# Two transformer blocks on one core: shorter norm chains, row sums on their own timer and queue, earlier weight splits, and the second mixer's norm chain issued inside its output projection

## The chip, the core and the metric

One core of a Trainium2 chip runs the whole program. Its engines each have a queue of their own and meet by semaphores: TensorE (PE) for matrix products and transposes, VectorE (DVE), ScalarE (ACT), GpSimd (POOL) and SyncE (SP, which issues DMAs). The metric is the device time of one execution in microseconds (us), the median of several runs. A trace of one execution, the profile, is at hand.

## What is computed

Two blocks, one after the other, over 256 positions of width 1024, all in float32. The first: a gated feed-forward (inner width 2816), a mixer with two attention branches, a second feed-forward. The second: a mixer with three branches (an mLSTM scan, a differential attention, a state space scan) that also looks at a 256-long context, and a feed-forward with a three-tap convolution over positions. Between them stands the residual with its norms:

```python
def rms_norm(x, g):
    xf = x.astype(jnp.float32)
    y = xf * lax.rsqrt(jnp.mean(xf * xf, axis=-1, keepdims=True) + EPS)
    return (y * g.astype(jnp.float32)).astype(x.dtype)

h = h + 0.5 * rms_norm(swiglu(rms_norm(h, ffn1_pre_g), ...), ffn1_post_g)
h = h + rms_norm(hybrid_mixer(rms_norm(h, mix_pre_g), ...), mix_post_g)
h = h + 0.5 * rms_norm(swiglu(rms_norm(h, ffn2_pre_g), ...), ffn2_post_g)
```

The second block is modulated: from the vector c six rows of 1024 are made, `silu(c) @ w_mod + b_mod` ("rows" below), which scale, shift and gate the normed input. `modulate(h, shift, scale)` is `h * (1 + scale) + shift`.

## The kernel before, in words

**Products.** Each float32 operand is split into a high and a low part in the fast format float32r; a product is three matmuls, hi x hi, hi x lo and lo x hi (lines 355 to 357 of `mm3`). Activations are kept transposed, `xT`, 128 features by 256 positions. A projection tile of 256 columns is 2 x 24 matmuls of about 0.12 us each. Expansions (`ffn_up`, `proj_fm`) write to PSUM from `psB`, `down` sums the result over all tiles for both blocks of 128 positions (`acc[tb]`, tb 0 and 1).

**Weights.** Class `Weights` loads pieces of 512 KB (`raw`, 5 buffers, SP's queue, L111) and splits each: `wh` on ACT (L126), `wl` on DVE (L127), into a ring of 4. `ahead` fills the ring as far as it may; `presplit` splits further pieces into general buffers (`u`).

**Order.** The order of all instructions is written out by hand: a clock counts the products that were issued (`tick`), and generators ("sides") are stepped when their time has come. In each tick the sides that were just made go first, then `ahead`, then the others. So an engine's queue holds weight splits, norm steps and row steps in the order of these ticks, and each waits in line. `heads` steps the attention heads of a mixer, in the first mixer every 2.6 us of this clock.

**The norm chains.** `residual_norm` makes the new residual and the next block's input: for each tb a generator `chain`, and a list `order` of what to step in each tick (0 and 1: the chains; 2 and 3: `to_T` of tb 0 and 1, eight transposes at L511, then hi on ACT at L346 and lo on DVE at L347). A chain squares on ACT with a running sum (L435), adds the two halves on DVE (L437), makes mean + eps (L421), takes the power -1/2 on POOL (L427), and scales on DVE (L459, L477, L479; L473 is the premultiplication by the gain where there is a shift; L456 and L464 multiply by the gain behind the down projection). While it runs, projections of the context (`ctx_attn`, `ctx_mlstm`, `ctx_ssd`) give TensorE work, one tick for each 24 products.

**The rows.** `mod_rows` is a side that adds up w_mod tiles on DVE (L981, L983), a step every `pace` us of the clock; after eight of them a generator `reduced` splits the sum (L346, L347), multiplies it by ones on TensorE (L957), adds bias and gain (L959, L961) and writes the row to DRAM. Its small DMAs go by SP; w_mod comes by ACT's queue (L975) into `v`, the pool of 12 buffers of 512 columns that heads and chains use, too.

**The second mixer** runs its heads in three groups, four mLSTM heads, eight attention steps and eight state space heads; `decay` (L1094 to L1107) makes for each scan head two tiles in `v`. Behind it `down("w_out_2", ...)` projects, and its norm chain is issued when that is through.

## Time and profile before

| | |
|---|---|
| median of three runs | 1230.99 us (1229.41 to 1232.49) |
| the profiled execution | 1230.0 us, its span 1228.2 us |
| busy TensorE, VectorE, ScalarE, GpSimd | 96%, 75%, 51%, 6% of the span |
| matmul instructions | 8728 |
| mean granted clock of TensorE | 0.989 of full speed |
| DMA | 251.33 MB, mean 205 GB/s |

The span runs from the first to the last instruction; the 1.8 us beside it lie around it. A row of a timeline gives the start in us, the duration, the engine, the line, the operation, what it writes and reads and how often, and in brackets the engine's idle time before it with what ended it. Starts of TensorE's rows are good, their ends are modelled. The granted clock is the share of full speed that TensorE was given; it has two levels, 1.2 and 2.4 GHz.

### The profile page before, as it was taken

How to read it: one execution, taken by the hardware profiler on the slowest of the kernel's cores; microseconds unless marked ns; L12 is line 12 of the kernel's file. 1: busy time of each engine (PE TensorE's matmuls, PEld its weight loads, DVE VectorE, ACT ScalarE, POOL GpSimd, SP SyncE). 2: the span in 40 equal slices, each digit the busy share in tenths (PEclk: the TensorE clock that was granted, in tenths of full speed). 3: DMA queues.
4: the chain of work that ended last, by engine and by line, in shares of the span. 5: the costliest groups of instructions: out<-in, count | busy, mean ns of one | idle time of the engine just before them, and what ended most of it. 6: DMA issues, size and time to landing. Idle time of an engine off the chain costs nothing. (4 is left out here: it accounts for less than half of the span.)

```text
span 1228.2 us, 22195 instructions
## 1 busy us (share of the span) xinstructions
PE 1184.8 (96%) x8728; PEld 1110.4 (90%) x8728; DVE 925.5 (75%) x1596; ACT 622.7 (51%) x1063; POOL 67.7 (6%) x84
## 2 busy tenths in 40 slices
PE   7999999998999988999999999999999998999998
PEld 7999988898978978999988899999898997999887
DVE  5798856666667869889886976698668777888854
ACT  4454545545556455454454654555566353555542
POOL 0020000100000000000000100055000000000000
PEclk8999999999999999999999999999999999999999
DMA  7888687576334776788888455446423384555572
GB/s 273 273 262 269 199 309 254 157 263 223 127 127 138 235 285 224 248 273 271 267 295 331 133 176 181 137 139 191 136 78 112 113 284 154 179 180 172 172 263 80
DMA packets 80644, 251.33 MB, mean 205 GB/s; under 512 B 9542, under 2 KB 10870, under 8 KB 80540
## 3 DMA queue, kind: packets, MB, share of 16 engines
q1 hardware_dynamic: 61692, 215.85, 52.0%
q10 hardware_dynamic: 18432, 33.56, 8.3%
q8 instruction: 68, 1.11, 0.4%
q0 software_dynamic: 416, 0.50, 0.3%
q14 instruction: 36, 0.29, 0.1%
HBM read 241.46 MB, written 8.42 MB: 203 GB/s over the span
## 5 line engine op out<-in xcount | busy, mean ns | idle before, releaser
L127 DVE TENSOR_TENSOR wl<-raw,wh 128x1024 fp32r<-128x1024 f32 (+3 forms) x358 | 423.6, 1218 | 129.6 <-ACT wh L126 124.9
L355 PE MATMUL pB<-u,wh 128*128 128x256 f32 x1696 | 486.2, 287 | 0.9 <-ACT u L346 0.9
L357 PE MATMUL pB<-u,wl 128*128 128x256 f32 x1696 | 482.0, 284 | 1.0 <-DVE wl L127 1.0
L356 PE MATMUL pB<-u,wh 128*128 128x256 f32 x1696 | 481.5, 284 | 0.8 <-DVE u L347 0.7
L126 ACT ACTIVATE wh<-raw 128x1024 fp32r<-128x1024 f32 (+3 forms) x358 | 358.8, 1046 | 97.5 <-PE pA L357 22.3
L355 PEld LDWEIGHTS pB<-u,wh 128*128 128x128 f32 x1696 | 326.5, 192 | 9.5 <-issue 7.2
L357 PEld LDWEIGHTS pB<-u,wl 128*128 128x128 f32 x1696 | 326.5, 193 | 2.3 <-DVE wl L127 1.4
L356 PEld LDWEIGHTS pB<-u,wh 128*128 128x128 f32 x1696 | 326.5, 193 | 2.0 <-DVE u L347 1.5
L355 PE MATMUL pB<-wh,u 128*128 128x512 f32 (+3 forms) x614 | 208.2, 339 | 1.6 <-ACT wh L126 1.6
L356 PE MATMUL pB<-wl,u 128*128 128x512 f32 (+3 forms) x614 | 206.9, 337 | 1.0 <-DVE wl L127 0.9
L357 PE MATMUL pB<-wh,u 128*128 128x512 f32 (+3 forms) x614 | 206.3, 336 | 0.0
L355 PEld LDWEIGHTS pB<-wh,u 128*128 128x128 f32 x614 | 117.4, 191 | 13.3 <-ACT wh L126 1.8
L356 PEld LDWEIGHTS pB<-wl,u 128*128 128x128 f32 x614 | 117.3, 191 | 13.3 <-DVE wl L127 2.5
L357 PEld LDWEIGHTS pB<-wh,u 128*128 128x128 f32 x614 | 117.1, 191 | 11.8
L519 ACT ACTIVATE w<-pB 128x256 f32<-128x256 f32 x44 | 16.9, 384 | 114.1 <-PE pB L357 113.7
L427 POOL TENSOR_TENSOR rs<-ms,nhalf 128x1 f32<-128x1 f32 (+2 forms) x30 | 29.2, 975 | 815.3 <-DVE ms L421 812.6
L983 DVE SCALAR_TENSOR_TENSOR v<-v,silu_c,v 128x512 f32<-128x512 f32 x84 | 62.4, 743 | 0.3
L1010 DVE SCALAR_TENSOR_TENSOR w<-pB,cols,w 128x255 f32<-128x255 f32 x120 | 49.6, 476 | 15.9 <-ACT w L1005 10.1
L520 DVE SCALAR_TENSOR_TENSOR w<-w,pB 128x256 f32<-128x256 f32 x44 | 18.5, 419 | 30.2 <-ACT w L519 30.2
L356 PE MATMUL pA<-wl,u 128*128 128x256 f32 x132 | 38.3, 290 | 1.8 <-DVE wl L127 1.8
L355 PE MATMUL pA<-wh,u 128*128 128x256 f32 x132 | 38.6, 292 | 0.9 <-ACT wh L126 0.9
L357 PE MATMUL pA<-wh,u 128*128 128x256 f32 x132 | 37.9, 287 | 0.0
(363 smaller groups left out, 1322.3 us busy)
## 6 DMA issues: line engine op xcount, KB each, us to landing
raw<-f_gu SPq DMA_DIRECT2D x88, 512.0 KB, 5.4
v<-w_mod ACTq DMA_DIRECT2D x128, 256.0 KB, 4.9
raw<-w_lat SPq DMA_DIRECT2D x64, 512.0 KB, 4.1
raw<-f_dn SPq DMA_DIRECT2D x44, 512.0 KB, 5.7
raw<-w_up_t SPq DMA_DIRECT2D x44, 512.0 KB, 5.1
raw<-w_ctx SPq DMA_DIRECT2D x22, 512.0 KB, 5.0
raw<-w_down_t SPq DMA_DIRECT2D x22, 512.0 KB, 5.1
raw<-w_in_g SPq DMA_DIRECT2D x16, 512.0 KB, 4.6
```

What stands on the lines that cost most here:

```text
L126: nc.scalar.activation(hi, r, AF.Copy)
L127: nc.vector.tensor_tensor(out=lo, in0=r, in1=hi.bitcast(F32), op=OP.subtract)
L355: nc.tensor.matmul(out, a[0], b[0], start=first, stop=False)
L356: nc.tensor.matmul(out, a[0], b[1], start=False, stop=False)
L357: nc.tensor.matmul(out, a[1], b[0], start=False, stop=last)
L427: self.nc.gpsimd.tensor_tensor(out=r, in0=ms, in1=self.nhalf[:, :width], op=OP.pow)
L519: nc.scalar.activation(th, p[:, 0], AF.Tanh, scale=0.5)
L520: nc.vector.scalar_tensor_tensor(th, th, 1.0, p[:, 0], op0=OP.add, op1=OP.mult)
L983: nc.vector.scalar_tensor_tensor(acc, ws[n - ahead], sc, acc, op0=OP.mult, op1=OP.add)
L1010: nc.vector.scalar_tensor_tensor(y[j][:, o], p[:, j, x], tap(t, i), y[j][:, o], op0=OP.mult, op1=OP.add)
```

## The change

- **Pools:** `v` has 10 buffers instead of 12; w_mod tiles get a pool of 5.
- **Norm chains:** squares are scaled so that their sums are means (`mean2`), and one DVE step adds both with eps (`rstd2`), where there were two. The chain with a norm has one more yield, and the orders interleave the two blocks otherwise and put the transposes a tick later.
- **Start:** the first gain comes as one row and is spread by TensorE; the second block's squares are taken on DVE; fewer warm-up products.
- **Heads:** the first step comes one pace after `heads` is called.
- **Rows:** each half's reduction is a side of its own, with two pauses of 2 us and then one tick from load and product to the addition; its small DMAs go by POOL's queue. In the second and third norm stage the row side is held off by 14 us. `need_rows` steps these sides too. The pace is 2.5 instead of 2.6 in the second feed-forward.
- **Early splits:** one piece each in two tiles of `w_out_t` and of the second `f2_dn`, two pieces at the last but one tile of the last expansion. The last `down` takes tb 0's sums from `psA` and tb 1's from `psB`.
- **Second mixer:** a hook in `down("w_out_2", ...)` issues tb 0's whole chain ahead of tb 1's last products, the first part of tb 1's chain and tb 0's transposes ahead of tb 1's last 256 columns, and the rest of tb 1's chain behind the products; tb 1's sums are in three parts (512, 256, 256). The end of `down`, `ahead`, comes after that, then tb 1's transposes.

```diff
-NV = 12
+NV = 10
...
-        side = self.side(run())
+        side = self.side(run(), pace)
...
+    def down(self, name, nt, hT, aside=None, late=1, cols=((512, 512), (512, 512)), first=None, hook=None):
+        ps = lambda tb, n: first if first and tb == 0 else self.psB if first or n == 512 else self.psA
+        acc = [[ps(tb, n)([128, n]) for n in cols[tb]] for tb in range(TB)]
...
+            order = [(k, *x) for k in range(2) for x in each] if i or first else [(k, *x) for x in each for k in range(2)]
...
         for tb in range(TB):
             for x in range(len(cols[tb])):
+                if hook:
+                    hook(acc, tb, x)
                 for m in range(late):
                     for k in range(2):
                         mm(w, k, 2 * (nt - late + m) + k, tb, x, m)
+        if hook:
+            hook(acc, TB, 0)
         self.weights.ahead()
...
+    def mean2(self, src):
+        nc, got = self.nc, []
+        for x in src:
+            got.append(self.sb([128, 1], "ssq", 8))
+            nc.scalar.activation(self.v([128, 512])[:, :x.shape[-1]], x, AF.Square, scale=D ** -0.5, accum_out=got[-1])
+        return got
+
+    def rstd2(self, m):
+        nc = self.nc
+        e, r = self.sb([128, 1], "mse", 6), self.sb([128, 1], "rs1", 6)
+        nc.vector.scalar_tensor_tensor(e, m[0], EPS, m[1], op0=OP.add, op1=OP.add)
+        nc.gpsimd.tensor_tensor(out=r, in0=e, in1=self.nhalf[:, :1], op=OP.pow)
+        return r
...
-    def residual_norm(self, acc, h, gpost, norm, gpre, shift, xT, order=((0, 0), (1,), (0, 1), (2,), (1,), (3,))):
+    def residual_norm(self, acc, h, gpost, norm, gpre, shift, xT, order=((0, 0, 1, 0, 1), (1, 0), (1,), (), (2,), (), (3,)), mid=None):
...
             if norm:
-                s = self.sumsq(acc[tb])
+                r = self.rstd2(self.mean2(acc[tb]))
+                yield
                 for hf in range(2):
                     nc.vector.tensor_tensor(out=x[hf], in0=acc[tb][hf], in1=self.halves(gpost)[hf], op=OP.mult)
-                r = self.rstd(s, D, 1)
+                yield
                 for hf in range(2):
                     nc.vector.scalar_tensor_tensor(y[hf], x[hf], r, y[hf], op0=OP.mult, op1=OP.add)
-                yield
-                s = self.sumsq(y)
+                m = self.mean2(y)
+                yield
             elif acc is not None:
+                m, c = [], 0
+                for a in acc[tb]:
+                    cc, c = slice(c, c + a.shape[-1]), c + a.shape[-1]
+                    nc.vector.tensor_tensor(out=t[tb][:, cc], in0=a, in1=gpost[:, cc], op=OP.mult)
+                    nc.vector.tensor_tensor(out=h[tb][:, cc], in0=t[tb][:, cc], in1=h[tb][:, cc], op=OP.add)
+                    m += self.mean2([h[tb][:, cc]])
+                    if len(m) == 3:
+                        s = self.sb([128, 1], "ssq", 8)
+                        nc.vector.tensor_tensor(out=s, in0=m[0], in1=m[1], op=OP.add)
+                        m = [s, m[2]]
+                    yield
+            elif tb:
+                m = []
                 for hf in range(2):
+                    m.append(self.sb([128, 1], "ssq", 8))
+                    nc.vector.scalar_tensor_tensor(x[hf], y[hf], 1.0 / D, y[hf], op0=OP.mult, op1=OP.mult, accum_out=m[-1])
             else:
-                s = self.sumsq(y)
-            r = self.rstd(s, D, 1)
+                m = self.mean2(y)
+            r = self.rstd2(m)
...
-            yield
+            if not norm:
+                yield
...
-    def ffn_up(self, name, xT, act):
+    def ffn_up(self, name, xT, act, early=0):
...
+            if f == NFF - 2:
+                self.weights.presplit(early)
...
         def reduced(acc, c, j, gain, hf):
             hi, lo = self.v([128, 512], F32R), self.v([128, 512], F32R)
             self.split(hi, lo, acc)
+            yield 2
+            yield 2
             x = self.v([1, 512])
-            nc.sync.dma_start(x, I["b_mod_2"][:, j * D + hf * 512:j * D + hf * 512 + 512])
+            nc.gpsimd.dma_start(x, I["b_mod_2"][:, j * D + hf * 512:j * D + hf * 512 + 512])
...
-            yield
             p = self.psA([128, 512])
...
-            nc.sync.dma_start(self.rows[c, j][:, hf * 512:hf * 512 + 512], x)
+            nc.gpsimd.dma_start(self.rows[c, j][:, hf * 512:hf * 512 + 512], x)
...
-                ws.append(self.v([128, 512]))
+                ws.append(self.sb([128, 512], "wm", 5))
...
-                    half.append(reduced(acc, c, j, gain, hf))
+                    half.append(self.side(reduced(acc, c, j, gain, hf)))
+                    self.row_sides = half[-2:]
...
+        gain = self.u([1, D])
+        nc.sync.dma_start(gain, I["ffn1_pre_g"])
...
-        self.warm_up(17)
-        t = self.residual_norm(None, h, None, False, g, None, xT, ((0, 0, 1), (1, 2), (3,)))
+        self.warm_up(4)
+
+        g, gain2 = self.u([128, D]), [self.psA([128, 512]) for _ in range(2)]
+        for hf in range(2):
+            nc.tensor.matmul(gain2[hf], self.ones[:1], self.halves(gain)[hf], start=True, stop=True)
+        self.warm_up(8)
...
+        t = self.residual_norm(None, h, None, False, g, None, xT, ((0, 1, 4, 0, 1, 2), (3,)), gains1)
...
-        acc = self.down("w_out_t", 4, mT)
+        acc = self.down("w_out_t", 4, mT, lambda i: self.weights.presplit(1) if i else None)
...
+        rows.ready += 14
...
-        pace[0] = 2.6
+        pace[0] = 2.5
...
+            if i in (8, 9):
+                self.weights.presplit(1)
...
-        t = self.residual_norm(acc, h, gp["post"], True, gp["pre"], gp["shift"], xT)
+        rows.ready += 14
+        t = self.residual_norm(acc, h, gp["post"], True, gp["pre"], gp["shift"], xT, ((0, 0, 1, 0, 1), (1, 0), (1,), (), (2,), (3,)))
...
-        acc = self.down("w_out_2", 4, mT, lambda i: self.weights.presplit(2 * i), 2)
-        t = self.residual_norm(acc, h, gp["post"], False, gp["pre"], gp["shift"], xT, ((0, 0, 0, 1, 1, 1, 0, 1, 2, 3),))
+        def hook(acc, tb, x):
+            if (tb, x) == (1, 0):
+                side.append(self.residual_norm(acc, h, gp["post"], False, gp["pre"], gp["shift"], xT,
+                                               ((0, 0, 0, 0), (1, 2), (1, 1, 1, 1), (3,))))
+            elif (tb, x) in ((1, 2), (2, 0)):
+                side[0].step()
+
+        self.down("w_out_2", 4, mT, lambda i: self.weights.presplit(2 * i), 2, ((512, 512), (512, 256, 256)), hook=hook)
+        self.join(*side)
...
-        hT = self.ffn_up("w_up_t", xT, self.conv_silu_mul)
+        hT = self.ffn_up("w_up_t", xT, self.conv_silu_mul, 2)
...
-        acc = self.down("w_down_t", NFF // 2, hT, None, 2, cols)
+        acc = self.down("w_down_t", NFF // 2, hT, None, 2, cols, first=self.psA)
```

## Rows read from the trace of the kernel before

**Rows 1.** Page, part 1: busy time, share of the span and instructions of each engine

```profile
PE 1184.8 (96%) x8728; PEld 1110.4 (90%) x8728; DVE 925.5 (75%) x1596; ACT 622.7 (51%) x1063; POOL 67.7 (6%) x84
```

**Rows 2.** Table of stretches: busy us (instructions), granted clock, DMA share, GB/s

```profile
220.00:240.00 20.00, 19.91 (x155) 19.67 (x155) 10.74 (x16) 10.19 (x17) 0.55 (x1) 0.91 0.42 138
...
300.00:320.00 20.00, 16.16 (x112) 15.71 (x111) 13.10 (x25) 6.13 (x13) 0.00 (x0) 0.83 0.40 133
...
480.00:500.00 20.00, 19.90 (x167) 19.48 (x166) 18.93 (x30) 9.94 (x17) 0.00 (x0) 1.00 0.82 281
```

**Rows 3.** Timeline of PE: start, us, form, count [idle before <- who ended it]

```profile
220.09 1.77 PE L511 MATMUL pB<-ident,u 128*128 128x128 f32 x8 [2.80 <-DVE u L477]
...
304.48 1.91 PE L829 MATMUL pA<-ident,u 128*96 128x128 f32 x8 [3.84 <-DVE u L690]
...
450.32 0.39 PE L356 MATMUL pA<-wl,u 128*128 128x256 f32 x1 [0.88 <-DVE wl L127]
...
463.63 1.97 PE L511 MATMUL pB<-ident,u 128*128 128x128 f32 x8 [3.91 <-DVE u L477]
...
687.80 1.32 PE L511 MATMUL pB<-ident,u 128*128 128x128 f32 x8 [1.76 <-DVE u L479]
...
1026.79 3.34 PE L511 MATMUL pB<-ident,u 128*128 128x128 f32 x16 [4.51 <-DVE u L479]
...
1166.95 0.50 PE L355 MATMUL pB<-wh,u 128*128 128x512 f32 x1 [1.57 <-ACT wh L126]
...
1168.21 0.50 PE L356 MATMUL pB<-wl,u 128*128 128x512 f32 x1 [0.76 <-DVE wl L127]
```

**Rows 4.** Timeline of DVE and of PE in the first 20 us

```profile
8.02 1.41 DVE L477 SCALAR_TENSOR_TENSOR u<-u,rs,u 128x512 f32<-128x512 f32 x2 [2.43 <-DMA u<-ffn_pre_g]
...
16.32 0.58 PE L356 MATMUL pB<-u,wh 128*128 128x256 f32 x1
```

**Rows 5.** Timeline of DVE in the first norm stage

```profile
219.29 1.41 DVE L477 SCALAR_TENSOR_TENSOR u<-u,rs,u 128x512 f32<-128x512 f32 x2
```

**Rows 6.** Timeline of DVE ahead of the first mixer's heads

```profile
299.39 2.36 DVE L127 TENSOR_TENSOR wl<-raw,wh 128x1024 fp32r<-128x1024 f32 x2 [5.06 <-ACT wh L126]
...
302.93 0.88 DVE L688 TENSOR_TENSOR w<-u,ropetab 128x128 f32<-128x128 f32 x4
```

**Rows 7.** Timeline of PE: the last product at the lower clock level

```profile
309.40 0.31 PE L355 MATMUL pB<-wh,u 128*128 128x256 f32 x1
```

**Rows 8.** Timeline of ACT and of DVE in the second norm stage

```profile
447.95 1.06 ACT L126 ACTIVATE wh<-raw 128x1024 fp32r<-128x1024 f32 x1 [5.67 <-DMA raw<-w_ctx]
...
457.71 0.74 DVE L983 SCALAR_TENSOR_TENSOR v<-v,silu_c,v 128x512 f32<-128x512 f32 x1
```

**Rows 9.** Timeline of ACT, then of PE, in the second mixer's scans

```profile
929.29 0.47 ACT L1106 ACTIVATE v<-pA,rcol 128x256 f32<-128x256 f32 x1
...
930.89 2.03 ACT L126 ACTIVATE wh<-raw 128x1024 fp32r<-128x1024 f32 x2
...
933.68 0.60 PE L1476 MATMUL pB<-w,u 128*64 128x256 f32 x4
...
935.13 0.29 PE L355 MATMUL pB<-u,wh 128*128 128x256 f32 x1
```

**Rows 10.** Timeline of DVE, then of PE, behind the second mixer

```profile
1012.72 2.51 DVE L127 TENSOR_TENSOR wl<-raw,wh 128x1024 fp32r<-128x1024 f32 x2
...
1016.88 0.69 DVE L464 TENSOR_TENSOR u<-pB,u 128x512 f32<-128x512 f32 x1 [0.31 <-PE pB L357]
...
1025.99 2.73 DVE L479 SCALAR_TENSOR_TENSOR u<-u,rs,u 128x512 f32<-128x512 f32 x4
...
1031.03 0.39 PE L356 MATMUL pB<-u,wh 128*128 128x256 f32 x1 [0.34 <-DVE u L347]
```

**Rows 11.** DMA issues: out<-in, queue, count, KB each, median us to landing

```profile
aqk_g<-a_knorm_g POOLq DMA_DIRECT2D x1, 32.0 KB, 8.1
...
rowbias<-m_fgate_b POOLq DMA_DIRECT2D x1, 4.0 KB, 4.2
```

More of the change, by code (lines that the diff above doesn't have):

```diff
@@ L387, in proj_tm @@
         return p
-    def down(self, name, nt, hT, aside=None, late=1, cols=((512, 512), (512, 512))):
-        acc = [[(self.psB if n == 512 else self.psA)([128, n]) for n in cols[tb]] for tb in range(TB)]
+    def down(self, name, nt, hT, aside=None, late=1, cols=((512, 512), (512, 512)), first=None, hook=None):
+        ps = lambda tb, n: first if first and tb == 0 else self.psB if first or n == 512 else self.psA
+        acc = [[ps(tb, n)([128, n]) for n in cols[tb]] for tb in range(TB)]
         def mm(w, k, kk, tb, i, m=0):
@@ L401, in down @@
             each = [(tb, x) for tb in range(TB) for x in range(len(cols[tb]))]
-            order = [(k, *x) for k in range(2) for x in each] if i else [(k, *x) for x in each for k in range(2)]
+            order = [(k, *x) for k in range(2) for x in each] if i or first else [(k, *x) for x in each for k in range(2)]
             for n, (k, tb, x) in enumerate(order):
@@ L488, in steps @@
                         next(c[tb])
+                    elif tb == 4:
+                        mid()
                     else:
@@ L497, in warm_up @@
     def warm_up(self, n):
-        self.ones = self.const([128, 128], "ones")
-        self.nc.vector.memset(self.ones, 1.0)
+        if not hasattr(self, "ones"):
+            self.ones = self.const([128, 128], "ones")
+            self.nc.vector.memset(self.ones, 1.0)
         p = self.psB([128, 128])
@@ L948, in reduced @@
             self.split(hi, lo, acc)
+            yield 2
+            yield 2
             x = self.v([1, 512])
-            nc.sync.dma_start(x, I["b_mod_2"][:, j * D + hf * 512:j * D + hf * 512 + 512])
+            nc.gpsimd.dma_start(x, I["b_mod_2"][:, j * D + hf * 512:j * D + hf * 512 + 512])
             if gain is not None:
                 g = self.v([1, 512])
-                nc.sync.dma_start(g, I[gain][:, hf * 512:hf * 512 + 512])
-            yield
+                nc.gpsimd.dma_start(g, I[gain][:, hf * 512:hf * 512 + 512])
             p = self.psA([128, 512])
@@ L968, in mod_rows @@
         half = []
-        for n in range(len(steps) + ahead + 3):
-            for h in half:
-                next(h, None)
+        for n in range(len(steps) + ahead):
             if n < len(steps):
                 (c, j, gain), hf, k = steps[n]
-                ws.append(self.v([128, 512]))
+                ws.append(self.sb([128, 512], "wm", 5))
                 nc.scalar.dma_start(ws[-1], I["w_mod"][j * 8 + k][:, hf * 512:hf * 512 + 512])
@@ L984, in mod_rows @@
                 if k == 7:
-                    half.append(reduced(acc, c, j, gain, hf))
+                    half.append(self.side(reduced(acc, c, j, gain, hf)))
+                    self.row_sides = half[-2:]
             yield -pace[0]
+        yield from self.until(*half)
     def need_rows(self, side, *keys):
         while not all(k in self.mods for k in keys):
-            side.step()
+            for s in list(self.row_sides):
+                while not s.done:
+                    s.step()
+            if not all(k in self.mods for k in keys):
+                side.step()
     def mod_bcast(self, c, j):
@@ L1148, in ctx_norm @@
         for tb, h in enumerate(hs):
-            r = self.rstd(self.sumsq(self.halves(h)), D, 1)
+            r = self.rstd2(self.mean2(self.halves(h)))
             yield 2
@@ L1663, in program, with gains1 @@
         xT = Split(self, 8)
-        self.warm_up(17)
-        t = self.residual_norm(None, h, None, False, g, None, xT, ((0, 0, 1), (1, 2), (3,)))
+        self.warm_up(4)
[3 more added lines that the diff above has]
+        self.warm_up(8)
+        def gains1():
+            for hf in range(2):
+                nc.vector.tensor_copy(self.halves(g)[hf], gain2[hf])
+        t = self.residual_norm(None, h, None, False, g, None, xT, ((0, 1, 4, 0, 1, 2), (3,)), gains1)
         self.weights.split()
@@ L1670, in program @@
         rope = self.side(self.rope_tables(), 40)
-        self.mods, self.rows = {}, {}
+        self.mods, self.rows, self.row_sides = {}, {}, []
         def setup():
@@ L1763, in program @@
         mT = self.mixer2(xT, aside)
-        acc = self.down("w_out_2", 4, mT, lambda i: self.weights.presplit(2 * i), 2)
         self.join(*gs)
-        xT, h = Split(self, 8), gp["h"]
-        t = self.residual_norm(acc, h, gp["post"], False, gp["pre"], gp["shift"], xT, ((0, 0, 0, 1, 1, 1, 0, 1, 2, 3),))
-        self.join(t)
+        xT, h, side = Split(self, 8), gp["h"], []
+        def hook(acc, tb, x):
[6 more added lines that the diff above has]
+        self.join(*side)
         back = self.spill(h, "res4")
         self.join(rows)
-        hT = self.ffn_up("w_up_t", xT, self.conv_silu_mul)
+        hT = self.ffn_up("w_up_t", xT, self.conv_silu_mul, 2)
         def last():
```

6 lines of the change are left out of this document (removed).

## The prediction

> **What bounds the kernel now.** The first view is busy time: TensorE works 1184.8 of 1228.2 us, 96%, VectorE 75%, ScalarE 51% [rows 1]. No product is added or taken away by the change but some at the start, so it can only win back TensorE's 43 idle us and the time at the lower clock level. The second view is the table of 20 us stretches: where TensorE was idle, the granted clock falls below 1.00 next to it [rows 2]. The third is TensorE's own timeline, read for rows with idle time in front [rows 3]. The long ones lie where one block ends and a norm chain has to turn the residual into the next input (transposes, L511): 2.80, 3.91, 1.76 and 4.51 us. Others: 3.84 in the first mixer, and 1.57 + 0.76 at the last down projection, both for weight splits. A 24-product group takes 24 x 19.90/167 = 2.86 us [rows 2]; this is what one "tick" of the hand-written order is worth, and the chains are hidden by counting such groups.
>
> The profiled execution took 1230.0 us, the median of three is 1230.99. I add the parts to 1230.0 and 1.0 at the end.
>
> **First input.** The gain row arrived as a 512 KB broadcast and the scaling waited 2.43 us for it, until 8.02; the second product came at 16.32 [rows 4]. Now 4 KB come and two products of TensorE spread them; x of the second block lands some 1.5 us sooner. But VectorE now also takes the second block's squares, copies the gain out of PSUM twice and does all four scalings ahead of the first lo half. Worked through with 0.7 us for each 512-column step (half of the 1.41 of [rows 4]), lo of the second block is ready near 15.1 instead of 16.3. **-1.0**, between -3 and +1.
>
> **First norm stage (near 220).** The new list of steps puts the transposes one group later: TensorE gets there at 217.29 + 2.86 = 220.15. The chain loses one small sum twice and is interleaved with the other block's; in the old one scaling began at 219.29 [rows 5], the new one should have its first half by 218.7. The idle 2.80 goes. The clock of 0.91 over these 20 us means 3.6 us at the half level [rows 2], and half of what TensorE did in them comes back: 1.7. **-4.5**, between -2.8 and -4.5. The added group is work that was there anyway; at the end of the stage the same amount less is left behind the transposes, enough for their two splits.
>
> **First mixer (near 304).** Both first steps of the heads ran in one tick: rotation on VectorE, then at once the transposes that need it. VectorE was in two weight splits until 301.75, then in a row step, and rotated from 302.93 [rows 6]; TensorE waited 3.84. With the pause the transposes come one group later, 2.86; VectorE has a row step less in front, as rows are summed on their own timer. What is left is 0 to 1. The clock of 0.83 is 6.8 us at half level [rows 2]; TensorE was at it from 304.48 to 309.40 [rows 3, 7], so 2.5 come back. **-5.5**, between -2.8 and -6.3. The wait of VectorE for the mask's DMA later in this mixer is untouched.
>
> **Second norm stage (450 to 464).** Two pairs of waits of about 0.9 us each for w_ctx splits (2.7 in all; one of 0.88 is shown) go, since these are split two tiles earlier. But each early split moves the ring on: two further pieces are now split at the end of the down projection, ahead of the chain in ScalarE's queue. ScalarE stood 5.67 us for raw w_ctx until 447.95 [rows 8]; two more 512 KB pieces land 1.3 to 1.9 us apart, so the chain begins some 3.2 us later than before. It is then shorter: the row steps (0.74 us and two like it) that lay in it are held off by 14 us, and the other block's first half no longer follows a split, together 3.7. TensorE arrives at 463.63 - 3.91 - 2.7 + 2.86 = 459.9 and the chain is ready near 463.1: 3.2 remain of 6.6. **-3.5**, between 0 and -6.6.
>
> **Third norm stage (near 688).** One group later again, with the row DMAs out of the way; raw pieces are there in time, for TensorE, not DMA, ends the splits in front. The 1.76 goes [rows 3], and 0.77 before the second block's transposes. **-2.5**, between 0 and -2.9.
>
> **Last down projection (1167).** Two pieces are split two tiles ahead, and the first block's sums lie in banks that are free. The 1.57 and 0.76 go [rows 3]; the two extra splits lie under the last two projections. **-2.3**, between 0 and -2.5.
>
> **Fewer general buffers (12 to 10).** w_mod gets five of its own, which helps where rows run. In the second mixer no rows run. At the third scan head, two x tiles, two score tiles, one attention output and six decay tiles are 11. The second decay tile (exponential at 929.29) then has to wait until the first pair's products are read, at 933.68 + 0.60; ScalarE's queue behind it, with the weight splits of 930.89, is 5.0 us late, and TensorE wants these at 935.13 [rows 9]: wh at 936.9, its lo half 1.2 later. **+2.8**, between 0 and +5.
>
> **Behind the second mixer (1012 to 1034).** This is where I see a loss. The first block's chain could begin in the old order too: its second product was done at 1016.88 [rows 10]; the new order starts it no earlier. It then runs to its scaling without a break: product and sum 2 x 0.69, square 0.8, sum 0.2, premultiplication 1.3, two scalings of 0.68 each, that is until 1021.9; its transposes go ahead of the last 256 columns. Only now comes the second block's first half on VectorE (0.69 + 0.69, to 1023.3), then its square on ScalarE, and the first block's hi halves stand behind that square, its lo halves behind those (to 1026.0); two 256-column pairs (1.7), square and sum (0.8), premultiplication (1.3), half a scaling: 1030.5. In the old order transposes began at 1026.79. And the two splits of w_up, 2.51 us at 1012.72 in an idle stretch ahead of the chain [rows 10], now stand behind the scaling and ahead of the second block's lo halves: 1031.15 + 2.4 + 0.65 = 1034.2 for the second product of the expansion, against 1031.03 [rows 10]. That is 3.2; the half level, which fell on transposes before, now falls on products: 1.7 more. **+5**, between -2 (the first block's transposes hidden, nothing else late) and +6.
>
> **Row steps on POOL's queue.** Sixteen half rows send their loads and stores by POOL instead of SP; the arithmetic stays. The load is issued one tick before VectorE reads it. POOL's loads of 4 and 32 KB landed after 4.2 and 8.1 us [rows 11], more than the 2.86 of a tick; but POOL is busy 6% of the span [rows 1] and waits for nothing but the buffer, so it can issue well ahead. I take 0 and keep the price for a rival. The Trainium skill speaks on both sides here: "DMA: Bandwidth & Descriptors" prefers the hardware queues in its specifications (about 0.6 against 1 us to the first byte), and fits such a transfer as 2.0 us plus bytes over 436 GB/s in "Anatomy of one DMA — SWDGE (gpsimd) path". By that fit, an estimate, a 2 KB load lands within the tick and nothing waits; the two rows say 4.2 and 8.1, and the measurement decides.
>
> **Sum.** -1.0 - 4.5 - 5.5 - 3.5 - 2.5 - 2.3 + 2.8 + 5 = -11.5, so 1230.0 - 11.5 = 1218.5, and with 1.0 for the median 1219.5; I say 1219.
>
> **The rivals.** (1) *The last chain is no loss and the buffers suffice:* VectorE finds the second block's first half ready and interleaves as it is meant to, as at the other norms. Without +2.8 and +5 it is 1211; with the -2 it is 1209. For: the product of the second block's first half is ready 2 us before VectorE is. Against: the queue is in order, and the sum above has hardly a gap on VectorE. (2) *The waits come back:* ScalarE stuck on raw pieces eats the second and third stage (6.0 back), the rotation hides half (2.7 less): 1228. For: the 5.67 wait in rows 8. Against: at 688 no DMA held the chain. (3) *POOL's loads hold VectorE, slower than before:* a load that is issued only with its step makes VectorE wait its landing less 2.86. In the expansions VectorE has 1.07 us idle in 20 [rows 2], some 1.2 between two half rows 23 us apart. At a landing of 6.2 each wait is 3.3, 2.1 reach TensorE, twelve times (those within the two feed-forwards): 25 us, 1244. It turns slower than before from a landing of 5.1 on, where 1.0 us times 12 eats the 11.5. What the Trainium skill prefers in "DMA: Bandwidth & Descriptors", the hardware queues, would be borne out by this. POOL's idleness speaks against it.
>
> **How the numbers follow.** Forecast 0.50 (its own range 1213 to 1225), rival 1 0.24, rival 2 0.19, rival 3 0.07. Faster or slower counts beyond 0.3%, 3.7 us, about what a measurement of this kernel can tell: below 1227.3, above 1234.7. Rival 2 lies astride the first bound, half of it on each side: faster 0.82, same 0.11, slower 0.07. The range 1208 to 1229 holds the forecast, most of rival 1 and of rival 2.
>
> **What would show it.** Right: at L511 near 220 and 688 no idle row, the clock 1.00 there; near 304 less than 1 us; near 460 a wait of 2 to 4; no wait for splits near 1167. At the second mixer's end TensorE idle for more than 4.51 in two pieces, and the two w_up splits between scaling and lo halves on VectorE. In the scans one decay exponential some 5 us behind its neighbour. Wrong: rows on VectorE waiting for b_mod loads by several us each (rival 3), or chain starts that follow a DMA (rival 2). What I would not see coming is a new wait where heads, rows and splits only shift by a group.

## The result and the profile after

The changed kernel takes 1216.54 us (median of four runs, 1216.02 to 1217.37) against 1231.42 for the kernel before in the same runs: a ratio of 0.9882 (95% interval 0.9865 to 0.9899), 14.9 us less. The forecast was 1219. The profiled execution has a span of 1214.6 us, 13.6 less than before.

Busy time by engine, from the first part of the page of the kernel after (it answers to [rows 1]):

```profile
PE 1183.6 (97%) x8746; PEld 1107.8 (91%) x8746; DVE 925.0 (76%) x1587; ACT 622.2 (51%) x1061; POOL 88.1 (7%) x122
```

The timeline of PE after, rows with idle time in front; they answer to [rows 3], and those at 13.52 and 14.99 to the product of [rows 4]:

```profile
13.52 0.39 PE L355 MATMUL pB<-u,wh 128*128 128x256 f32 x1 [0.73 <-ACT u L346]
14.99 0.38 PE L356 MATMUL pB<-u,wh 128*128 128x256 f32 x1 [1.09 <-DVE u L347]
...
296.13 1.05 PE L870 MATMUL pA<-ident,u 128*96 128x128 f32 x8 [0.37 <-DVE u L731]
...
355.80 1.24 PE L771 MATMUL pB<-ident,v 128*128 128x128 f32 x8 [1.28 <-DVE v L764]
...
434.88 0.39 PE L356 MATMUL pA<-u,u 128*128 128x256 f32 x1 [0.88 <-DVE u L127]
...
446.05 1.32 PE L549 MATMUL pB<-ident,u 128*128 128x128 f32 x8 [0.95 <-DVE u L512]
...
450.06 0.39 PE L357 MATMUL pA<-u,wl 128*128 128x256 f32 x1 [1.02 <-DVE wl L127]
...
673.34 0.39 PE L357 MATMUL pA<-u,wl 128*128 128x256 f32 x1 [1.59 <-DVE wl L127]
...
917.87 0.71 PE L1140 MATMUL pA<-ecs,pick 128*128 128x256 f32 x2 [0.83 <-DVE w L1503]
...
921.17 0.78 PE L1458 MATMUL pA<-ident,v 128*128 128x128 f32 x4 [2.59 <-ACT v L1153]
922.73 0.58 PE L355 MATMUL pB<-u,wh 128*128 128x256 f32 x1 [0.78 <-ACT u L346]
...
1005.74 1.23 PE L549 MATMUL pB<-ident,u 128*128 128x128 f32 x8 [0.27 <-DVE u L514]
...
1014.38 1.97 PE L549 MATMUL pB<-ident,u 128*128 128x128 f32 x8 [6.00 <-DVE u L514]
...
1017.92 0.58 PE L356 MATMUL pB<-u,wh 128*128 128x256 f32 x1 [1.15 <-DVE u L347]
...
1160.28 0.50 PE L356 MATMUL pA<-wl,u 128*128 128x512 f32 x1 [0.20 <-DVE wl L127]
```

Four of the waits of [rows 3] are gone or nearly so: TensorE has no idle time in front of the transposes (now L549) of the first and the third norm stage, which begin at 217.00 and 669.05, and in the last projection one wait of 0.20 for a split is left (1160.28) of 1.57 + 0.76. The 3.84 in the first mixer is 0.37 (at 296.13; L870 is the old L829), and 3.91 became 0.95. Two places got worse: the end of the second mixer (0.27 + 6.00 + 1.15, where 4.51 + 0.17 + 0.34 stood) and the scans, at 917.87 to 922.73.

The table of 20 us stretches after (as in [rows 2]: busy us of PE, PEld, DVE, ACT, POOL, then the granted clock, DMA share, GB/s) shows the same from the clock's side:

```profile
220.00:240.00 20.00, 20.00 (x176) 20.00 (x175) 12.09 (x15) 9.97 (x16) 2.91 (x1) 1.00 0.76 246
300.00:320.00 20.00, 20.00 (x157) 18.87 (x156) 17.28 (x33) 11.71 (x28) 0.00 (x0) 1.00 0.50 162
920.00:940.00 20.00, 17.91 (x128) 14.79 (x129) 15.77 (x38) 10.53 (x25) 0.00 (x0) 0.83 0.26 85
1000.00:1020.00 20.00, 12.58 (x68) 10.81 (x67) 15.99 (x28) 9.14 (x18) 1.88 (x2) 0.76 0.21 62
1020.00:1040.00 20.00, 20.00 (x154) 20.00 (x154) 11.66 (x21) 8.32 (x15) 0.00 (x0) 0.90 0.63 217
```

In the stretches from 220 and from 300 the clock is now 1.00 where [rows 2] has 0.91 and 0.83. In the scans it fell to 0.83, where the kernel before had no stretch below 1.00, and behind the second mixer to 0.76 and 0.90, where the kernel before had one stretch at 0.91.

For each stage the gain can be read from the shift of one instruction between the two traces: the first product of w_out_t starts at 425.43 before and at 410.26 after, so 15.2 us were won up to there. The table does this for every stage, from the median shift of the instructions in the quiet stretches between them (and from that product):

| stage | forecast | measured |
|---|---|---|
| first input (to 170) | -1.0 | -3.0 |
| first norm stage | -4.5 | -4.7 |
| first mixer (to the first product of w_out_t) | -5.5 | -7.4 |
| second norm stage | -3.5 | -4.1 |
| third norm stage | -2.5 | -2.4 |
| scans (fewer general buffers) | +2.8 | +6.0 |
| behind the second mixer | +5.0 | +5.3 |
| last down projection | -2.3 | -3.1 |
| sum | -11.5 | -13.4 |

The -3.0 of the first line is not all from the start: from the 49th product of the first expansion (23.35 before, 20.90 after) the shift is 2.4 to 2.5, and 0.6 more comes near 94, where the product of a row (L957) waited for its split in the kernel before:

```profile
93.73 0.39 PE L957 MATMUL pA<-v,onesr 128*1 128x512 f32 x1 [0.42 <-DVE v L347]
```

Every sign came as forecast. The gains are larger than forecast by 5.4 us in all and the losses by 3.5; that the sum is so close is partly luck, as these cancel.

### The profile page after: what moved, and what is told of

Its sections match the earlier page's. It is cut to its first block, busy times and chain, and to the rows that moved or that the text cites. A ratio compares the mean times of both kernels' runs of the same rounds, so it can differ in the third digit from the quotient of the medians.

```text
span 1214.6 us, 22306 instructions
## 1 busy us (share of the span) xinstructions
PE 1183.6 (97%) x8746; PEld 1107.8 (91%) x8746; DVE 925.0 (76%) x1587; ACT 622.2 (51%) x1061; POOL 88.1 (7%) x122
## 5 line engine op out<-in xcount | busy, mean ns | idle before, releaser
L127 DVE TENSOR_TENSOR wl<-raw,wh 128x1024 fp32r<-128x1024 f32 (+3 forms) x352 | 416.8, 1218 | 115.9 <-ACT wh L126 111.8
L126 ACT ACTIVATE wh<-raw 128x1024 fp32r<-128x1024 f32 (+3 forms) x352 | 352.9, 1046 | 72.3 <-PE pB L357 37.4
L355 PE MATMUL pB<-wh,u 128*128 128x256 f32 (+3 forms) x594 | 194.9, 328 | 0.0
L357 PE MATMUL pB<-wh,u 128*128 128x256 f32 (+3 forms) x594 | 193.6, 326 | 0.0
L356 PE MATMUL pB<-wl,u 128*128 128x256 f32 (+3 forms) x594 | 193.6, 326 | 0.0
L355 PEld LDWEIGHTS pB<-wh,u 128*128 128x128 f32 x594 | 112.9, 190 | 10.3 <-issue 0.7
L356 PEld LDWEIGHTS pB<-wl,u 128*128 128x128 f32 x594 | 112.8, 190 | 9.6
L357 PEld LDWEIGHTS pB<-wh,u 128*128 128x128 f32 x594 | 112.8, 190 | 9.5
L1023 DVE SCALAR_TENSOR_TENSOR v<-wm,silu_c,v 128x512 f32<-128x512 f32 x84 | 62.6, 745 | 0.3
L356 PE MATMUL pA<-wl,u 128*128 128x256 f32 (+1 forms) x132 | 42.0, 318 | 0.3 <-DVE wl L127 0.2
L355 PE MATMUL pA<-wh,u 128*128 128x256 f32 (+1 forms) x132 | 42.0, 318 | 0.0
L357 PE MATMUL pA<-wh,u 128*128 128x256 f32 (+1 forms) x132 | 41.6, 315 | 0.0
L346 ACT ACTIVATE u<-w 128x256 fp32r<-128x256 f32 x22 | 9.2, 418 | 55.1 <-DVE w L573 55.1
```

Of the source, the lines that this page charges most:

```text
L126: nc.scalar.activation(hi, r, AF.Copy)
L127: nc.vector.tensor_tensor(out=lo, in0=r, in1=hi.bitcast(F32), op=OP.subtract)
L346: nc.scalar.activation(hi, src, AF.Copy)
L355: nc.tensor.matmul(out, a[0], b[0], start=first, stop=False)
L356: nc.tensor.matmul(out, a[0], b[1], start=False, stop=False)
L357: nc.tensor.matmul(out, a[1], b[0], start=False, stop=last)
```

## The experiments

All runs are the changed kernel with one edit. Times are ratios to the kernel before, measured beside it, and in brackets what the ratio makes of 1231.42. "By the trace" is the shift of the instructions behind the stage against the changed kernel's trace, less the shift ahead of it. One trace of each kernel is kept, and traces differ where the code does not, too: by -0.4 to +0.6 us over the scans in nine runs that leave these as they are, and by 0 to -1.4 us behind the second mixer in eight (there the changed kernel's own trace, with one other, is the slowest). The first input is spoken of in the last section.

**The decay tiles take another pool.**

```diff
 def decay(self, r, d):
-    E = self.v([128, 384])
+    E = self.sb([128, 512], "wm", 5)[:, :384] if d == 0 else self.v([128, 384])
```

> The changed kernel, but the first of each scan head's two decay tiles takes a buffer of the w_mod pool (5, unused since 669 us) instead of the general pool of 10. Theory (the general pool is too small at the third state space head, and the wait set off an idle stretch and then the lower clock level): the exponential at 911.08 no longer waits 3.44 us for the first pair's products, the idle 0.83 + 2.59 us of TensorE at 917.87 and 921.17 fall to at most 0.4 each, the granted clock stays 1.00 up to 1010, and about 6.0 us come back: 1210.5 us (1209.5 to 1211.5). Rival (the loss in the scans is from the order of the steps, not from the buffers): 1216.5 us (1215.5 to 1217.5), the idle rows stay.

Measured: 0.9837, 0.9813 to 0.9861 (1211.3); by the trace -6.1. The timeline of ACT in the scans of the changed kernel:

```profile
911.08 0.47 ACT L1152 ACTIVATE v<-pA,rcol 128x256 f32<-128x256 f32 x1 [3.44 <-PE pB L1522]
...
912.70 2.01 ACT L126 ACTIVATE wh<-raw 128x1024 fp32r<-128x1024 f32 x2
...
920.08 0.42 ACT L1624 ACTIVATE u<-u 128x256 f32<-128x256 f32 x1 [4.12 <-DVE u L1623]
```

and of its DVE:

```profile
913.80 2.36 DVE L127 TENSOR_TENSOR wl<-raw,wh 128x1024 fp32r<-128x1024 f32 x2 [0.55 <-ACT wh L126]
...
917.39 0.75 DVE L1503 TENSOR_TENSOR w<-pA,u 128x256 f32<-128x256 f32 x2
...
919.62 0.43 DVE L1623 SCALAR_TENSOR_TENSOR u<-u,u 128x256 f32<-128x256 f32 x1
```

The exponential at 911.08 waits 3.44 us for the products of the first pair (L1522) to give back their buffers. The weight splits behind it (912.70, then 913.80 on DVE) push the scaling of the next decays to 917.39, and that and the attention's steps put L1623 at 919.62, for which ScalarE waits another 4.12. TensorE is hit at 917.87 and again at 921.17. The same place with the other pool, in PE's timeline of this run:

```profile
918.59 0.66 PE L1458 MATMUL pA<-ident,v 128*128 128x128 f32 x4 [0.35 <-ACT wm L1153]
```

and in its table of stretches (columns as above):

```profile
920.00:940.00 20.00, 19.66 (x169) 16.61 (x170) 18.18 (x38) 9.94 (x21) 0.00 (x0) 1.00 0.29 88
```

The wait of 2.59 is 0.35, the clock 1.00. So the waits come from the buffers. The clock behind them is less sure: the run with both losses taken away (below) has the same short waits here and still 3.4 us at the lower level, and its shift over the scans is -4.5. The buffers therefore cost 4.5 to 6.1 us.

**The second mixer's chain behind its projection again.**

```diff
-        def hook(acc, tb, x): ...
-        self.down("w_out_2", 4, mT, ..., 2, ((512, 512), (512, 256, 256)), hook=hook)
+        acc = self.down("w_out_2", 4, mT, lambda i: self.weights.presplit(2 * i), 2)
+        t = self.residual_norm(acc, h, ..., xT, ((0, 0, 0, 1, 1, 1, 0, 1, 2, 3),))
```

> The changed kernel, but the second mixer's norm chain is issued behind the output projection as before the change (sums in two parts of 512 for both blocks, the old list of steps); the new arithmetic of the chain stays. Theory (issuing it inside the projection puts the second block's chain and the two splits of w_up in line behind the first block's chain, which costs 5.3 us): 1211.2 us (1210 to 1212.5), TensorE's idle in front of the second block's transposes 4.0 to 4.6 us instead of 6.00, the stretch at the lower clock level 3 to 4 us instead of 13.7. Rival 1 (the new chain steps or the other placement of what precedes are the loss, not the place of issue): 1216.5 us (1215.5 to 1217.5). Rival 2 (the place of issue is worth what it was made for, and undoing it costs): 1218 us or more.

Measured: 0.9851, 0.9823 to 0.9878 (1213.1); by the trace -5.5, and the span is 5.9 shorter. The ratio gives less, 3.4 us, and lies above the expected range, since the profiled execution was the fastest of four (1210.70; the others 1212.65 to 1213.70). From the timeline of PE in this run:

```profile
1010.50 3.36 PE L549 MATMUL pB<-ident,u 128*128 128x128 f32 x16 [4.32 <-DVE u L514]
...
1014.73 0.38 PE L356 MATMUL pB<-u,wh 128*128 128x256 f32 x1 [0.34 <-DVE u L347]
```

of its DVE:

```profile
997.00 2.49 DVE L127 TENSOR_TENSOR wl<-raw,wh 128x1024 fp32r<-128x1024 f32 x2
```

and of DVE in the changed kernel:

```profile
1008.86 1.29 DVE L347 TENSOR_TENSOR u<-pB,u 128x512 fp32r<-128x512 f32 x2 [1.27 <-ACT u L346]
1010.06 0.41 DVE L488 TENSOR_TENSOR u<-pA,u 128x256 f32<-128x256 f32 x1
...
1013.58 1.41 DVE L514 SCALAR_TENSOR_TENSOR u<-u,rs,u 128x512 f32<-128x512 f32 x2
1014.91 2.36 DVE L127 TENSOR_TENSOR wl<-raw,wh 128x1024 fp32r<-128x1024 f32 x2
1017.18 1.28 DVE L347 TENSOR_TENSOR u<-pB,u 128x512 fp32r<-128x512 f32 x2
```

In the changed kernel the first block's lo halves (1008.86) stand in front of the second block's last sums (1010.06), and the two splits of w_up (1014.91, 2.36 us) between its scaling and its lo halves (1017.18). Undone, these splits are done at 997.00, in an idle stretch, and the wait is 4.32. Issuing the chain inside the projection is a loss, of 3.4 us by the ratio and 4 to 5.5 by the traces; rival 1 and rival 2 of this run fall.

**Only the two splits ahead of the chain.**

```diff
         w = self.weights.take(name, nt - late, late)
+        if hook:
+            self.weights.ahead()
```

> The changed kernel with one line more: the two splits of w_up are issued ahead of the first block's chain (they stand in line there when the chain is undone), the chain stays inside the projection. Theory (these splits, 2.36 us on VectorE between the second block's scaling and its lo halves, are the part of the loss that delays the second product): the second product of the expansion comes some 1.6 us earlier and 0.8 us of the lower clock level with it, 1214 us (1213 to 1215.5); the idle 6.00 us in front of the transposes stays within 0.3. Rival 1 (ahead of the chain they delay the first block's sums and with them the transposes): 1217 us or more, the idle above 6.5 us. Rival 2 (the splits are free where they are): 1216.5 us.

Measured: 0.9872, 0.9848 to 0.9895 (1215.7); by the trace -2.2, with 5.99 us in front of the transposes as in the changed kernel and no wait at the second product, where 1.15 stood. The medians don't separate this from no change and lie just above the expected range. In the trace the wait of 1.15 went, and the lower level lasts 6.8 us where it lasts 13.7 in the changed kernel's trace; but it lasts 10.2 in seven of the eight traces with the same code at this place. So the splits' place is worth some 1 to 2 of the 5.3 us. That the rest is the chain behind the first block's lo halves, and the clock, is argued from the rows above.

**Both losses taken away.** The first two edits together.

> The changed kernel with the two edits that gained most: the first of each scan head's decay tiles from the w_mod pool, and the second mixer's norm chain issued behind the projection. Theory (two separate losses, 5.6 and 5.9 us by the spans): span 1214.6 - 11.5 = 1203.1, 1205 us (1203.5 to 1206.5), no stretch at the lower clock level between 900 and 1000. Rival (the two losses share a cause, such as TensorE's state after the scans, and do not add): 1208 us or more.

Measured: 0.9794, 0.9766 to 0.9821 (1206.1), below every run of the changed kernel (1205.89 to 1210.99 against 1216.02). The losses add; this version beats both kernels. One expectation failed: there is a stretch at the lower level in the scans (923.6 to 927.0), though the long waits there are gone.

**The heads' first step at once.**

```diff
-        side = self.side(run(), pace)
+        side = self.side(run())
```

> The changed kernel, but the heads' first step comes at once again, as before the change. Theory (the pause of one pace is what took the wait in front of the first mixer's head transposes away): a wait of 2.5 to 4 us comes back there with 6 to 7 us at the lower clock level, 1216.5 + 5.5 = 1222 us (1220 to 1223). Rival (the rows' own timer, which takes a row step out from in front of the rotation, did it, the pause did nothing): 1216.5 to 1217.5 us, a wait under 1 us.

Measured: 0.9942, 0.992 to 0.9963 (1224.3); by the trace +6.6. PE's timeline of this run:

```profile
296.61 1.05 PE L870 MATMUL pA<-ident,u 128*96 128x128 f32 x8 [3.25 <-DVE u L731]
...
354.15 0.58 PE L998 MATMUL pA<-v,onesr 128*1 128x512 f32 x1 [3.50 <-DVE mx L749]
```

The first wait is the 3.84 of [rows 3] come back, at 3.25. The second was not expected: VectorE stands 6.4 us for the mask's DMA (4.5 in the kernel before, 1.2 in the changed one), and TensorE 3.50 behind it. The pause took both away; with the mask the price is above the range expected. The rival, that the rows' own timer did it, falls.

**The rows' small DMAs by SP.**

```diff
-            nc.gpsimd.dma_start(x, I["b_mod_2"][...])
+            nc.sync.dma_start(x, I["b_mod_2"][...])
```

(and so for the gain and the store)

> The changed kernel, but the rows' small loads and stores are issued by SP's queue again instead of POOL's; their own timer stays. Theory (the queue is worth nothing either way, because VectorE's waits for these loads are hidden under TensorE's work): 1216.5 us (1215.5 to 1217.5). Rival 1 (SP issues late, behind weight loads that wait for a buffer, and VectorE stands for it): waits of VectorE at the bias addition of 2 us and more each, 16 of them, 1219 us or more. Rival 2 (POOL's loads land too late and cost something now): 1214.5 us or less, and VectorE's idle in front of the bias addition is smaller than in the changed kernel.

Measured: 0.9991, 0.9977 to 1.0005 (1230.3); +14.9 by the span. All of the change's gain is gone: an edit that looked free decides over it. The view of the line that adds the bias (L1001; what its engine sat idle for: us, times), of this run:

```profile
  DMA v<-b_mod: 35.5, 9
```

and of the kernel before (L959):

```profile
  DMA v<-b_mod: 4.4, 4
```

In the changed kernel that view has no such row. Its loads (the list of DMA issues: count, KB, median us to landing)

```profile
v<-b_mod POOLq DMA_DIRECT2D x16, 2.0 KB, 4.0
```

land after 2.3 to 7.9 us, in the median after more than a tick, but POOL issues each 10.9 us or more ahead of its use (mostly 17 to 30); by SP, where it is issued behind weight loads that wait for their buffers, the lead is 3.1 to 11.0 us, in the kernel before 3.3 to 16.3 (the leads are from the timelines).

So the theory fell and rival 1 holds, with 9 waits instead of 16: the queue is worth 14.9 us to the new timer. The edit moves the stores, too, and no run separates these from the loads; the waits that the trace shows are for loads. The Trainium skill gives simple loads to SP's queue ("DMA: Bandwidth & Descriptors", section "Issuing engine by pattern"); weighed in the prediction, this is not borne out here, because of what stands ahead in that queue. By its fit (section "Anatomy of one DMA — SWDGE (gpsimd) path") a 2 KB load by POOL takes 2.0 us, an estimate; that is half of the median of 4.0 in this trace.

**All of the row code as before.** The old `reduced`, stepped with the row steps, and the old `need_rows`; the w_mod pool and the 14 us of delay stay.

> The changed kernel with the row code of the kernel before (reduction stepped with the row steps, small DMAs by SP, the old way of asking for rows); the w_mod pool of 5 and the 14 us for which rows are held off stay. Theory (the new timer alone would cost 14.9 us, as the run with SP showed, and POOL's queue takes just that back, so that together they are worth nothing): 1216.5 us (1215.5 to 1218), VectorE's waits for the bias 3 to 6 us in all, TensorE reached by none above 1 us. Rival 1 (POOL's queue is worth many us of itself): 1222 us or more. Rival 2 (the row step that no longer stands in front of the first mixer's rotation is part of the first mixer's gain): 1218 to 1221 us, with a wait of 1 to 2 us in front of the first mixer's head transposes.

Measured: 0.9933, 0.9909 to 0.9958 (1223.2); by the trace +0.5 in the first mixer (0.96 in front of the heads' transposes instead of 0.37) and +7.0 between 515 and 710. The cause of the latter is one load. DVE in this run:

```profile
638.28 0.68 DVE L1000 TENSOR_TENSOR v<-pA,v 1x512 f32<-1x512 f32 x1 [9.14 <-DMA v<-b_mod]
```

and PE:

```profile
640.81 0.80 PE L356 MATMUL pB<-wl,u 128*128 128x512 f32 x1 [4.34 <-DVE wl L127]
```

SP issues it at 630.03, behind the broadcasts for the next norm, and TensorE's 4.34 us bring the lower clock level with them (0.85 in the stretch from 640). That the rows come due just there because they are held off by 14 us is argued, not shown. The theory of this run (no difference) fell: the row part is worth some 7 us to the changed kernel. What it would be worth to the kernel before was not run; there a row made TensorE wait only once, the 0.42 us at 93.73.

**The old start.** Gain as a broadcast, 17 warm-up products, the old steps (the fragment of the change's diff reversed).

> The changed kernel with the start of the kernel before (gain as a 512 KB broadcast, 17 warm-up products, its list of steps, the second block's squares on ScalarE). Theory (the new start is worth 1.3 us of waiting and 1.7 us of the lower clock level, which fell on the first products): 1219.5 us (1218.5 to 1220.5), about 6.8 us at the lower level around 12 to 19 us. Rival (as forecast, the waiting alone counts): 1217.5 us.

Measured: 0.9901, 0.9877 to 0.9924 (1219.2); by the trace +3.4. In the first 20 us the granted clock is 0.76 in this run, 1.00 in the changed kernel's trace. The second product comes at 17.34 instead of 14.99; the other 1.1 us is lost behind it, at the lower level. The rival's 1217.5 lies within the interval of the ratio; it is the trace, with this stretch, that speaks against it. Not all of the 3.4 is the old start's: in the kernel before the second product came at 16.32 [rows 4], 1.0 earlier than here, since the second block's x landed earlier (ScalarE squares it from 8.60 there and from 9.61 here). Against that trace the new start gains 2.4 to 2.5.

**No early splits in w_out_t.**

```diff
-        acc = self.down("w_out_t", 4, mT, lambda i: self.weights.presplit(1) if i else None)
+        acc = self.down("w_out_t", 4, mT)
```

> The changed kernel without the two early splits in the tiles of w_out_t. Theory (an early split also frees its load buffer early, so the loads behind it leave sooner and the chain of the second norm stage began only 1.3 us later for it, while two pairs of waits for w_ctx went): the four waits of 0.7 to 0.9 us come back, the chain starts 1.3 us earlier and no longer makes the transposes wait, so 1217 to 1218.5 us. Rival 1 (as forecast: the two extra pieces hold the chain by 3.2 us, so without them the transposes come as much earlier as the splits cost): 1216 us (1215 to 1216.5). Rival 2 (the early splits bring all of the stage's gain): 1221 us or more.

Measured: 0.9889, 0.9864 to 0.9914 (1217.8); by the trace +0.8. The chain's first square starts 1.8 us earlier (434.32 instead of 436.12) and the transposes wait for nothing, as the theory has it; of the split waits 0.90 and 0.88 stand in front of the w_ctx products, where the changed kernel has 0.88 alone, so one came back and not four. Even that one can't be put down to the edit: the run with the decay tiles' other pool, which keeps these early splits, has 0.70 and 0.88 there, a stretch at the lower level as this run has (0.93 from 420 there, 0.92 here), no wait at the transposes and a shift of +0.7. The run shows no gain from the two early splits. The delay of the chain in the changed kernel's ACT timeline:

```profile
432.51 1.06 ACT L126 ACTIVATE u<-raw 128x1024 fp32r<-128x1024 f32 x1 [6.42 <-DMA raw<-w_ctx]
433.87 1.06 ACT L126 ACTIVATE wh<-raw 128x1024 fp32r<-128x1024 f32 x1 [0.30 <-DMA raw<-w_ctx]
435.15 1.06 ACT L126 ACTIVATE wh<-raw 128x1024 fp32r<-128x1024 f32 x1 [0.22 <-DMA raw<-w_ctx]
436.12 0.58 ACT L452 ACTIVATE v<-pB 128x512 f32<-128x512 f32 x1
```

Three pieces are split ahead of the chain's first square (436.12), where the kernel before had one [rows 8]; they come 1.3 us apart.

**The first norm's transposes a group earlier.**

```diff
-        t = self.residual_norm(acc, h, gp["post"], True, gp["pre"], None, xT)
+        t = self.residual_norm(..., ((0, 0, 1, 0, 1), (1, 0), (1,), (2,), (), (), (3,)))
```

> The changed kernel, but in the first norm stage alone the first block's transposes are issued one group of 24 products earlier, as before the change; the steps of the chain stay. Theory (the first scaled half is ready at 214.95, and TensorE would be there at 217.0 - 2.86 = 214.1; the chain itself became some 2 us shorter): a wait of 0.8 to 1.0 us in front of these transposes, no stretch at the lower clock level, 1217.3 us (1216.5 to 1218). Rival (as forecast, the later place alone pays: the old wait of 2.80 us with the lower level): 1221 us or more.

Measured: 0.9884, 0.986 to 0.9909 (1217.1); the wait in this run (PE):

```profile
217.20 1.32 PE L549 MATMUL pB<-ident,u 128*128 128x128 f32 x8 [0.46 <-DVE u L512]
```

0.46, not 2.80, and the clock around it is 1.00; by the trace the earlier place costs 0.9. So the shorter, interleaved chain by itself takes nearly all of the wait away. The later place with the old chain was not run; by the prediction's sum (2.86 against 2.80) it would have done so, too.

**The last projection as before.** Without `early=2` and `first`.

> The changed kernel without the two early splits at the last expansion and with the last projection's sums and its first tile's order as before. Theory (this part is worth the two waits for splits, 1.57 + 0.76 us, and little more): 1216.5 + 2.3 to 3.0 = 1219 us (1218 to 1220), the two waits are there again. Rival (the loads of the last weights end last, and the waits go elsewhere): 1216.5 us.

Measured: 0.9912, 0.989 to 0.9934 (1220.6); by the trace +3.0, with the two waits of [rows 3], 1.57 and 0.76, back to the hundredth. The ratio gives 4.1, just above the expected range. The rival falls; what makes up the other 0.7 in the trace was not found.

No run was made of four parts by themselves: the 14 us by which rows are held off, the pool of five for w_mod, the early splits in the second `f2_dn` with the pace of 2.5, and the later transposes of the third norm stage.

## Why the prediction was right, and where it was not

**First input.** The wait was sized right (the second product 1.3 us earlier, at 14.99), the clock was left out. The trace of before is at the lower level from 12.5 to 19.3, the one of after is not, and in the products behind the second another 1.1 us came back. The step that failed is a missing term, the same that I did count at the two stages next to it. The other 0.6 of the stage lies near 94 and belongs to the rows.

**First norm stage.** -4.7 as forecast, but the sum holds two causes of which either would nearly do. I let TensorE arrive 2.86 later at a chain that was a little shorter. Its scaling begins 2.1 us earlier (214.23, against 219.29 - 3.0 in [rows 5]), and the run with the earlier place shows that this alone leaves 0.46 to wait. How much the later place would have done without it stays open.

**First mixer.** The mechanism was right, and the run without the pause shows it. The step that failed is the sentence that the mask's wait is untouched: the pause moves the reading of the mask, too. That wait of TensorE went, another of 1.28 came near it (355.80), and the lower clock level behind it (364.0 to 367.4 in the trace of before) with it. These and the terms I had add up to 8.6 us; where 1.2 of them went was not traced.

**Second norm stage.** The terms were right and both a little off. Shifted by the 15.2 us won so far, the chain starts 2.4 us later than before (1.8 later than without the early splits) where I took 3.2, since the pieces land 1.3 apart; and from its first square to the first scaled half it takes 9.9 us where it took 14.7, 4.8 less where I took 3.7. So 0.95 remains at the transposes instead of 3.2; but 0.88 of the split waits stayed, and 1.02 at a split behind the transposes I did not see coming.

**Third norm stage.** As forecast in size and partly by luck: the 1.76 and the 0.77 went, but a split behind the transposes, which waited 0.39 before, now waits 1.59 (673.34). The waits fell by 1.3 us and not by the 2.4 of the shift; what makes up the rest was not traced.

**Last projection.** The two waits were the right ones, and the run without this part has them back; it gave 0.7 more than forecast.

**Scans.** The cause (the second decay tile of the third head waits for a buffer, and the weight splits queue behind it) was right, and so was the idle time: the waits of the stretch are 4.56 us against 1.72 before (0.30, 0.39, 0.69 and 0.34), 2.8 more. Where TensorE waits was not. I had it wait for the late weight splits at the product of 935.13 in [rows 9]; that product comes at 913.42 now, without idle time. The late splits held VectorE instead, and TensorE waited 4 to 8 us further on, for the scaling (917.87) and a later exponential (921.17). So the agreement on 2.8 is luck. The term that failed is the clock: in stretches of 1 us it is at the lower level from 921.6 to 928.4, with 5.9 us of work in them, and half of that is 3.0. The bound of +5 was the delay of one split; it had no clock in it.

**Behind the second mixer.** The idle time came in pieces (0.27, 6.00 and 1.15), the splits lie between scaling and lo halves, the second product comes 2.6 us later against the forecast 3.2, and the lower level lasts longer (1010.3 to 1024.0, with 8.5 us of work): the step held as written, and rival 1 fell. The price is 5.3 for 5 in this trace, and up to 1.4 less in others with the same code.

**Rows by POOL.** I had taken the queue for an edit of no price. The stage table leaves little for it against the kernel before (some 0.6 us near 94), but that is the sum of two large terms: with the new timer and SP's queue the loads come too late (14.9 us), and POOL's lead pays for it. The reason given for 0 (POOL waits for nothing but the buffer) agrees with the leads. Rival 3 fell by that lead. Rival 2 fell with the second norm stage.

## What to carry to other kernels

Where TensorE will wait, price the wait and then the half speed behind it: in the scans the second was as large as the first. Price an edit together with those it lives with: a queue that looks free may be what another edit needs. Where two edits could each remove the same wait, run each alone before crediting one. And before issuing a chain earlier, list what the queue then holds in front of the next one that TensorE will wait for.

## What the runs showed of the hardware

The lower clock level comes in some executions of nearly the same code and not in others. With the new start, waits of about 1 us in front of the first two products stand in every trace; the first 20 us have a granted clock of 1.00 in eight of eleven traces and 0.91 in three. The 49th product starts at 20.6 to 21.3 us in the eight and at 23.0 to 23.3 in the three, against 23.35 in the kernel before: with the lower level the new start gains 0.0 to 0.4 us instead of 2.0 to 2.7. The stretch in the changed kernel:

```profile
0.00:20.00 20.00, 16.96 (x85) 13.14 (x86) 12.77 (x23) 8.59 (x13) 2.37 (x7) 1.00 0.69 237
```

and, with two later ones, in the run with both losses taken away:

```profile
0.00:20.00 20.00, 16.73 (x68) 13.52 (x69) 13.13 (x23) 8.64 (x13) 2.52 (x7) 0.91 0.66 227
360.00:380.00 20.00, 19.81 (x141) 16.67 (x141) 13.71 (x43) 11.60 (x29) 0.48 (x1) 0.91 0.40 132
920.00:940.00 20.00, 18.62 (x141) 15.48 (x141) 16.70 (x40) 11.33 (x25) 0.00 (x0) 0.91 0.26 88
```

That profiled execution took 1210.99 us, the other three of the same kernel 1205.89 to 1207.62. In the last of these stretches the waits are 0.35, 0.69 and 0.34 us, as in the run with the decay tiles' other pool alone, where the clock stayed at 1.00. A small idle stretch therefore has no fixed price, and where one profile is compared with another, the shift has to be read stage by stage with the clock beside it.
